# A three-layer forward pass on one core: key and value products put into the heads' pipeline steps, and two small stages moved one step later

## The chip, the cores and the metric

The kernel runs on one core of a Trainium2 chip. The metric is the device time of one execution in microseconds (us). Before the change it is 1878.92 us, the median of 3 runs (1877.95 to 1881.15).

## The reference

A sequence of 512 tokens of width 1024 passes through three mixers, each followed by a feed-forward part. The first mixer is a gated linear recurrence with a convolution of width 4, the second is attention over latent keys with a learned choice of keys, the third is chunked gated linear attention with a pooling branch. The change touches the first and the second. Cut to what matters there:

```
# recurrence: convolution, two gates, scan, output product
gate, xr = split(h @ w_in, 2);  gate = gelu(gate)
xc = conv_b + sum_k xpad[:, k:k+S] * conv_w[k]
r = sigmoid(xc_blocks @ w_a + b_a);  i = sigmoid(xc_blocks @ w_x + b_x)
log_a = -8 * r * softplus(-lam);  a = exp(log_a);  u = sqrt(-expm1(2*log_a)) * (i * xc)
hs = scan(hs*a + u);  y = (hs * gate) @ w_out

# attention: q (16 heads of 64), latent c (128), index queries and keys
c = rms_norm(c, kv_norm_g)
score = sum_h wi_h * relu(qi_h . ki);  idx = top_k(score, 128), per query
logits = q_lat . c[idx] + bias;  p = softmax(logits);  o_lat = p @ c[idx]
o = (o_lat @ w_uv) @ w_o          # q_lat = (q @ w_uk) / 8
```

The kernel multiplies the latent keys by `w_uk` and `w_uv` once (key products `kt`, value products `v`), and takes the choice of keys as a mask that is added to the logits.

## The kernel before

All activations lie transposed, features on 128 partitions and 512 tokens along a row. Every product runs in three matmuls of rounded operands (`group`, lines 348 to 353: high by high, low by high, high by low), so each weight chunk of 128x1024 is split first: ScalarE (ACT) rounds it into `wh` (line 254), VectorE (DVE) or, in the attention, GpSimd (POOL) subtracts to get `wl` (line 255). Activations are split in the same way by `split` (lines 364 and 365). A matmul's result stands in one of eight PSUM banks (`PS`, one pool of eight tiles), and a new product takes the bank of the one eight earlier, once that has been read out.

The order of the work is made by `run` (line 268 on). A job is a list of stages, and job i executes its stage s in step i + s: in each step stage 0 of the newest job comes first, then the later stages of older jobs. A scheduler then lays the instructions out for each engine by priority, so an instruction can move a little, but each engine then works strictly in its order. A stage that waits on an engine holds everything behind it there.

The recurrence. `LAYER0` lists its jobs: eight convolution tiles `xr` 0 to 7 (`conv_job`: product; read-out `xr`; taps, one on ACT and three on DVE, into `xc`; rounding `out_`), four gate pairs `ax` 0 to 3 (`recur_job`: 24 matmuls into four banks; gates `rg` and `ig` on ACT, lines 570 and 571; factors; scan `hs`), and eight output gates `rgate` (24 matmuls each; gelu; product with `hs`; rounding `h`, `l` from `gate`). The rounding of the last tile, `xr` 7, belongs to the same step as the gates of `ax` 1, and stands ahead of them on ACT. `ax` 2 needs the banks that `ax` 1's gates read out; the tile `xr` 7 itself is first needed by `ax` 3. The output product `rout` then reads the eight rounded tiles of `gate`, in order.

The attention. First come the index queries, the keys, the query products `q_job` (read out into `qq`) and the latent keys `c_job` (product; read-out `c` with its squares `csq`; an empty stage; `norm`, a sum over partitions by a matmul `tot` and a reciprocal square root; `out_`, rounding into `C`). The top-k choice runs on DVE as 48 rounds (lines 809 and 810, 16 for each of three query blocks), handed out a few at a time by the jobs. Then 8 key products `kt_job` (3 matmuls, read out by ACT into `kth` and by DVE into `ktl`, then three DMAs on SyncE's queue (SP) into `kto` and `kth`), 8 value products `v_job` (3 matmuls, read out by ACT and DVE into `vv`), and 32 heads `head_job` (16 heads for each half of the queries). A head has nine stages: loads (bias tile `btile`, query copies `qd` by DMA on SP, rounding `qph`, `qpl`); logits; softmax (DVE `probs`, `negmax`; ACT exponent; DVE `sums`; POOL scaling); top-k rounds; two empty ones; transposes `pT`, rounded into `pTh` and `pTl`; an empty one; value products `o`, read out for two heads at once (ACT `olo`, DVE `os`). All jobs stand in one list, one per step: key products 0 and 1, value products 0 and 1, then heads 0 and 1 with the last two query products, then for heads 2 to 4 each head followed by two key and two value products, then heads 5 to 31 alone.

Of the kernel before, what the change touches and what calls it, by code (L numbers as in the profile page):

```python
# [21 lines left out]
KD = D // P  # L22
# [193 lines left out]
def blocks(ap):  # L216
    return ap.rearrange("p (n c) -> p n c", c=P)


def reverse(ap):  # L220
    return blocks(ap)[:, :, ::-1]
# [49 lines left out]
def run(jobs):  # L271

    deep = max(len(j) for j in jobs)
    for step in range(len(jobs) + deep - 1):
        for stage in [0] + list(range(deep - 1, 0, -1)):
            i = step - stage
            if 0 <= i < len(jobs) and stage < len(jobs[i]):
                jobs[i][stage]()


@with_exitstack
def build(ctx, tc, xT, wall, par, relb, onehot, edges, out):
    nc = tc.nc
# [11 lines left out]
    def T(dt=F32, name="t"):  # L295
        return tp.tile([P, S], dt, name=name, tag="t")
# [25 lines left out]
    def pc(name, j=0, n=1):  # L322
        if name == "g_mix0":
            return g0[:, j:j + n]
        c = PCOL[name] + j
        return pt[:, c:c + n]
# [28 lines left out]
    def lin(X, *key):  # L355
        h, l = W.get(*key)
        ps = PS()
        group(ps, [(h[:, k * P:(k + 1) * P], l[:, k * P:(k + 1) * P], X[k][0], X[k][1]) for k in range(KD)])
        return ps

    def split(t):

        h, l = T(F32R, "h"), T(F32R, "l")
        act(h, t, AF.Copy)
        V.tensor_sub(l, t, h.bitcast(F32))
        return h, l
# [9 lines left out]
    def total(acc):  # L376
        ps = PS("tot")
        PE.matmul(ps, ones, acc, start=True, stop=True)
        return ps

    def rsqrt_mean(ps, n):
        s = T(name="std")
        act(s, ps, AF.Sqrt, scale=1.0 / n, bias=eps_t)
        V.reciprocal(s, s)
        return s
# [28 lines left out]
    def residual_job(j, mm, feed, half=False):  # L414
        st = {}

        def first():
            st["ps"] = mm()

        def second():  # L420
            if half:
                stt(xs[j], st["ps"], 0.5, xs[j], op0=ALU.mult, op1=ALU.add)
            else:
                V.tensor_add(xs[j], xs[j], st["ps"])  # L424
            if feed is not None:
                feed.add(xs[j])

        return [first, second]
# [82 lines left out]
    def first_products():  # L511

        first_ps.extend(PS() for _ in range(NFIRST))
        at = {f: i for i, f in enumerate(FIRST)}
        todo = sorted((max(at["x", k], at["w", c, k // 4]), k, c) for k in range(KD) for c in range(NFIRST))
        left = [3 * KD] * NFIRST
        for _, k, c in todo:
            (h, l), (xh, xl) = W.done[c], feed.X[k]
            cols = slice(k * P, (k + 1) * P)
            for a, b in ((h, xh), (h, xl), (l, xh)):  # L520
                left[c] -= 1
                PE.matmul(first_ps[c], a[:, cols], b, start=left[c] == 3 * KD - 1, stop=left[c] == 0)  # L522
        for c in range(NFIRST):
            W.get("xr", c)

    def conv_job(j):
        st = {}

        def mm():
            if j == 0:  # L530
                first_products()
            st["ps"] = first_ps[j] if j < NFIRST else lin(feed.X, "xr", j)

        def evict():
            t = st["t"] = T(name="xr")
            feed.r
            with tc.high_priority(offset=EARLY):
                V.tensor_mul(t, st["ps"], feed.r)

        def taps():  # L540
            t = st["t"]
            c = xc[j] = T(name="xc")
            act(c, t, AF.Identity, scale=pc("conv_w3", j), bias=pc("conv_b", j))
            for k in range(3):
                n = 3 - k
                stt(c[:, n:], t[:, :S - n], pc(f"conv_w{k}", j), c[:, n:], op0=ALU.mult, op1=ALU.add)

        def out_():
            xcs[j] = split(xc[j])

        return [mm] + [lambda: None] * max(0, 2 - j) + [evict, taps, out_]

    def recur_job(b):
        st = {}
# [91 lines left out]
    jobs = [[lambda: None, softplus]]  # L646
# [5 lines left out]
    def rout(j):  # L652

        if j == 0:
            rout_ps.extend(PS() for _ in range(4))
            for kk in range(4):
                h, l = W.get("routk", kk)
                for k in range(2):
                    kt = 2 * kk + k
                    yh, yl = Y[kt]  # L660
                    for i in range(4):
                        c = slice(k * 512 + i * P, k * 512 + (i + 1) * P)
                        PE.matmul(rout_ps[i], h[:, c], yh, start=kt == 0, stop=False)
                        PE.matmul(rout_ps[i], h[:, c], yl, start=False, stop=False)
                        PE.matmul(rout_ps[i], l[:, c], yh, start=False, stop=kt == KD - 1)
        return rout_ps[j] if j < 4 else lin(Y, "rout", j)

    jobs = [residual_job(j, lambda j=j: rout(j), nxt) for j in range(KD)]
# [28 lines left out]
    def qi_job(j):  # L697
        st = {}

        def mm():  # L700
            st["ps"] = lin(feed.X, "att", j)

        def ev():
            t = st["t"] = T(name="qi")
            V.tensor_mul(reverse(t), blocks(st["ps"]), blocks(feed.r))

        def out_():
            for e in range(2):
                qi[2 * j + e] = T(F32R, "qis")
                stack(qi[2 * j + e], st["t"], e, V if j == 0 else G)  # L710

        return [mm, ev, out_]
# [31 lines left out]
    def c_job():  # L744
        st = {}

        def mm():
            st["ps"] = lin(feed.X, "att", 5)

        def ev():  # L750
            c = st["c"] = T(name="c")
            V.tensor_mul(c, st["ps"], feed.r)
            sq = st["sq"] = T(name="csq")
            act(sq, c, AF.Square)

        def norm():
            st["r"] = rsqrt_mean(total(st["sq"]), P)

        def out_():
            c = st["c"]  # L760
            stt(c, c, pc("g_kv"), st["r"], op0=ALU.mult, op1=ALU.mult)
            C.extend(split(c))

        return [mm, ev, lambda: None, norm, out_]

    accs, ready = [None] * 4, [False] * 4

# [48 lines left out]
    def q_job(j):  # L816
        st = {}

        def mm():
            st["ps"] = lin(feed.X, "att", 6 + j)  # L820

        def ev():
            t = QF[j] = T(name="qq")
            stt(reverse(t), blocks(st["ps"]), 0.125, blocks(feed.r), op0=ALU.mult, op1=ALU.mult)

        def more():
            for _ in range(SELECT_PER_Q):
                next(rounds, None)

        return [mm, ev, more]  # L830

    def kt_job(j):
        st = {}

        def mm():
            if j == 0:
                uk.extend(W.get("uk"))
            ps = st["ps"] = PS()
            group(ps, [(uk[0][:, j * P:(j + 1) * P], uk[1][:, j * P:(j + 1) * P], *C)])

        def ev():
            h, l, o = T(F32R, "kth"), T(F32R, "ktl"), T(F32R, "kto")
            act(h, st["ps"], AF.Copy)
            V.tensor_sub(l, st["ps"], h.bitcast(F32))

            for dst, src in ((o[0:64], h[64:P]), (o[64:P], l[64:P]), (h[64:P], l[0:64])):
                nc.sync.dma_start(dst.bitcast(F32), src.bitcast(F32))
            KT[2 * j], KT[2 * j + 1] = h, o

        return [mm, ev]  # L850
# [145 lines left out]
    jobs = [qi_job(j) for j in range(4)] + [kw_job(), q_job(0)]  # L996
# [11 lines left out]
    heads = [head_job(pair, h) for pair in range(2) for h in range(16)]  # L1008

    kts = [kt_job(j) for j in range(8)]  # L1010
    vals = [v_job(kt, n) for kt, n in ((0, 0), (1, 0), (0, 1), (1, 1), (2, 0), (3, 0), (2, 1), (3, 1))]
    jobs += kts[:2] + vals[:2] + [heads[0], q_job(6), heads[1], q_job(7)]
    for i in range(2, 8, 2):
        jobs += [heads[i // 2 + 1]] + kts[i:i + 2] + vals[i:i + 2]

    def further():
        W.limit = len(W.plan)
        W.fetch(W.at + W.ahead)

    run(jobs + heads[5:10] + [[further]] + heads[10:])  # L1020

    nxt = Feed("g_mlp1")

# [48 lines left out]
    def lr_job():  # L1072
        st = {}

        def mm():
            st["ps"] = lin(feed.X, "lr")

        def ev():
            t = T(name="lr")
            V.tensor_mul(t, st["ps"], feed.r)  # L1080
            LR.extend(split(t))

        return [mm, ev]
# [315 lines left out]
    jobs = [lr_job(), [lambda: None, halves], k_job(0), k_job(1), k_job(2)]  # L1399
# [114 lines left out]
    jobs = [last_job(d, full, first, n, hid) for d in range(KD - 4)]  # L1514
# [39 lines left out]
```

## Time and profile before

| | us |
|---|---|
| median of 3 runs | 1878.92 |
| the profiled execution | 1878.08 |
| its span, first to last instruction | 1876.1 |
| TensorE (PE) busy | 1838.0 |
| DVE busy | 1020.1 |
| ACT busy | 807.4 |
| POOL busy | 201.4 |

The recurrence lies at about 7 to 150 us of the span, the attention with its heads at about 550 to 735 us. A busy PE in the profile is one that has a matmul under way; a 128x512 matmul is listed with 0.39 us, but the next one starts 0.23 us after it, since they overlap. The granted clock (PEclk) says how much of its full speed TensorE was given in a stretch. A row of a timeline gives the start in us from the beginning of the span, the duration, engine and line, and in brackets the idle time of the engine just before, with what ended it.

### The profile page before, as it was taken

To read this page: it belongs to the slowest core of one execution; us is meant where nothing else is said; L and a number is where in the kernel's file an instruction comes from. 1 tells how busy PE (TensorE), PEld (TensorE's weight loads), DVE (VectorE), ACT (ScalarE), POOL (GpSimd) and SP (SyncE) were. 2 spreads that over 40 slices of the span, in tenths; PEclk is the share of its full clock that TensorE was granted. 3 is DMA by queue.
4 is the path that set the end of the run, shared out by engine and by line. 5 is a ranking of instruction groups with operands and counts; after the bars stand their busy time and mean duration, and the time that the engine had idled before them with its cause. 6 is when DMAs were issued, how large, how long until landed. Compare 5 with 4: busy or idle time off the path is not lost.

```text
span 1876.1 us, 21800 instructions
## 1 busy us (share of the span) xinstructions
PE 1838.0 (98%) x8450; PEld 1522.8 (81%) x8450; DVE 1020.1 (54%) x1504; ACT 807.4 (43%) x1224; POOL 201.4 (11%) x202
## 2 busy tenths in 40 slices
PE   9899999999999689999999999999999999999998
PEld 7788888888887578888888888888888888888887
DVE  7787542443359987543244444736585554344344
ACT  6794431343344586442134445356542333122233
POOL 0000000000165465000000023401000000000000
PEclk9999999999999899999999999999999999999999
DMA  5223222222233531222222222221122222222221
GB/s 200 84 90 103 101 90 101 96 96 101 90 101 111 143 90 40 101 99 92 101 93 99 101 90 100 92 90 57 60 98 94 97 100 92 101 95 95 102 75 60
DMA packets 60999, 179.36 MB, mean 96 GB/s; under 512 B 7696, under 2 KB 18144, under 8 KB 60896
## 3 DMA queue, kind: packets, MB, share of 16 engines
q1 hardware_dynamic: 60752, 177.97, 28.1%
q8 instruction: 66, 1.08, 0.2%
q14 instruction: 37, 0.30, 0.1%
q10 hardware_dynamic: 144, 0.00, 0.0%
HBM read 168.48 MB, written 2.12 MB: 91 GB/s over the span
## 4 chain that ended last, share of the span: by engine, by line
PE 91%; DVE 5%; ACT 2%; DMA 1%; issue 1%; POOL 0%; SPq 0%; DVEq 0%; ACTq 0%; POOLq 0%
PE ps L351 19%; PE ps L353 19%; PE ps L352 19%; PE dn L352 8%; PE dn L353 8%; PE dn L351 8%; DVE score L810 1%; PE o L1317 1%; DVE top L809 1%; PE ps L522 1%; PE v L1222 1%; PE v L1223 1%; PE v L1224 1%; DVE score L791 1%; PE kv L1291 1%
## 5 line engine op out<-in xcount | busy, mean ns | idle before, releaser
L254 ACT ACTIVATE wh<-wst 128x1024 fp32r<-128x1024 f32 (+2 forms) x314 | 328.0, 1046 | 897.3 <-PE ps L352 364.0
L351 PE MATMUL ps<-xh,wh 128*128 128x512 f32 x1376 | 540.8, 393 | 0.0
L353 PE MATMUL ps<-xh,wl 128*128 128x512 f32 x1376 | 535.3, 389 | 0.0
L352 PE MATMUL ps<-xl,wh 128*128 128x512 f32 x1376 | 535.2, 389 | 0.0
L255 DVE TENSOR_TENSOR wl<-wst,wh 128x1024 fp32r<-128x1024 f32 (+2 forms) x283 | 342.6, 1211 | 221.6 <-ACT wh L254 194.8
L352 PEld LDWEIGHTS ps<-xl,wh 128*128 128x128 f32 x1376 | 258.3, 188 | 55.9 <-issue 2.4
L351 PEld LDWEIGHTS ps<-xh,wh 128*128 128x128 f32 x1376 | 258.3, 188 | 55.5 <-issue 2.2
L353 PEld LDWEIGHTS ps<-xh,wl 128*128 128x128 f32 x1376 | 258.3, 188 | 53.7
L351 PE MATMUL dn<-h,wh 128*128 128x512 f32 (+1 forms) x712 | 271.8, 382 | 0.0
L352 PE MATMUL dn<-l,wh 128*128 128x512 f32 (+1 forms) x712 | 271.7, 382 | 0.0
L353 PE MATMUL dn<-h,wl 128*128 128x512 f32 (+1 forms) x712 | 271.7, 382 | 0.0
L255 POOL TENSOR_TENSOR wl<-wst,wh 128x1024 fp32r<-128x1024 f32 x31 | 75.8, 2452 | 916.6 <-ACT wh L254 916.4
L351 PEld LDWEIGHTS dn<-h,wh 128*128 128x128 f32 x712 | 133.8, 188 | 26.1
L352 PEld LDWEIGHTS dn<-l,wh 128*128 128x128 f32 x712 | 133.8, 188 | 25.9
L353 PEld LDWEIGHTS dn<-h,wl 128*128 128x128 f32 x712 | 133.8, 188 | 25.7
L424 DVE TENSOR_TENSOR x<-x,dn 128x512 f32<-128x512 f32 x48 | 33.0, 688 | 170.7 <-PE dn L353 170.7
L455 DVE SCALAR_TENSOR_TENSOR relu<-ps,std 128x512 f32<-128x512 f32 x64 | 44.2, 691 | 146.8 <-PE ps L353 146.7
L351 PE MATMUL ps<-h,wh 128*128 128x512 f32 x200 | 78.7, 396 | 5.4 <-ACT rg L570 5.4
L352 PE MATMUL ps<-l,wh 128*128 128x512 f32 x200 | 78.8, 394 | 0.0
L353 PE MATMUL ps<-h,wl 128*128 128x512 f32 x200 | 78.6, 393 | 0.0
L351 PEld LDWEIGHTS ps<-h,wh 128*128 128x128 f32 x200 | 38.0, 190 | 14.5 <-ACT rg L570 6.3
L1501 DVE TENSOR_TENSOR u<-ps,std 128x512 f32<-128x512 f32 x22 | 15.2, 690 | 62.5 <-PE ps L353 62.5
(315 smaller groups left out, 2128.2 us busy)
## 6 DMA issues: line engine op xcount, KB each, us to landing
wst<-wall SPq DMA_DIRECT2D x300, 512.0 KB, 3.2
btile<-biasdram SPq DMA_DIRECT2D x32, 128.0 KB, 3.1
qd<-qq SPq DMA_DIRECT2D x64, 64.0 KB, 2.2
wst<-wall SPq DMA_DIRECT2D x8, 384.0 KB, 2.9
x<-xT SPq DMA_DIRECT2D x8, 256.0 KB, 5.2
out_dram<-fin SPq DMA_DIRECT2D x8, 256.0 KB, 2.3
wst<-wall SPq DMA_DIRECT2D x6, 256.0 KB, 5.1
kto<-kth SPq DMA_DIRECT2D x8, 128.0 KB, 3.0
```

The lines of the kernel that those rows point to most:

```text
L254: self.nc.scalar.activation(h[:, a:b], st[:, a:b], AF.Copy)
L255: eng.tensor_sub(l[:, a:b], st[:, a:b], h[:, a:b].bitcast(F32))
L351: PE.matmul(ps, wh, xh, start=i == 0, stop=False)
L352: PE.matmul(ps, wh, xl, start=False, stop=False)
L353: PE.matmul(ps, wl, xh, start=False, stop=i == n - 1)
L424: V.tensor_add(xs[j], xs[j], st["ps"])
L455: stt(t, st["ps"], 0.0, feed.r, op0=ALU.max, op1=ALU.mult)
L522: PE.matmul(first_ps[c], a[:, cols], b, start=left[c] == 3 * KD - 1, stop=left[c] == 0)
L791: stt(accs[i][:, :w], d[:, :w], sg, accs[i][:, :w], op0=ALU.mult, op1=ALU.add)
L809: V.max(top, acc[:, :w])
L810: V.match_replace(acc[:, :w], top, acc[:, :w], MARK)
L1222: PE.matmul(st["ps"][i], xh, hk, start=kt == 0, stop=False)
```

## The change

Four edits, all of them in which step a stage falls.

The rounding of the convolution's last tile gets an empty stage ahead of it. The norm of the latent keys gets a second empty stage ahead of it. A new function `together` merges jobs into one that executes their stages of the same number in one step. With it, key products 0 and 1 share a step; value products 0 and 1 share the step of head 0's loads; then query product 6; head 1 with key products 2 and 3; query product 7; and heads 2 to 6 each with two more products (value 2 and 3; key 4 and 5; key 6 and 7; value 4 and 5; value 6 and 7). Heads 7 to 31 stand alone as before. No instruction is added or taken away.

```
+def together(*jobs):
+
+    deep = max(len(j) for j in jobs)
+    return [lambda n=n: [j[n]() for j in jobs if n < len(j)] for n in range(deep)]
...
-        return [mm] + [lambda: None] * max(0, 2 - j) + [evict, taps, out_]
+        return [mm] + [lambda: None] * max(0, 2 - j) + [evict, taps] + [lambda: None] * (j == KD - 1) + [out_]
...
-        return [mm, ev, lambda: None, norm, out_]
+        return [mm, ev, lambda: None, lambda: None, norm, out_]
...
-    jobs += kts[:2] + vals[:2] + [heads[0], q_job(6), heads[1], q_job(7)]
-    for i in range(2, 8, 2):
-        jobs += [heads[i // 2 + 1]] + kts[i:i + 2] + vals[i:i + 2]
+    jobs += [together(*kts[:2]), together(heads[0], *vals[:2]), q_job(6), together(heads[1], *kts[2:4]), q_job(7)]
+    beside = (vals[2:4], kts[4:6], kts[6:8], vals[4:6], vals[6:8])
+    jobs += [together(heads[i + 2], *b) for i, b in enumerate(beside)]
...
-    run(jobs + heads[5:10] + [[further]] + heads[10:])
+    run(jobs + heads[7:10] + [[further]] + heads[10:])
```

The lines of the changed kernel are counted six higher from `run` on. On ACT, in the recurrence, this stands before the gates of `ax` 1 (`rg`, `ig`), first before the change:

```order
L614 ACTIVATE gate<-gate 128x512
L254 ACTIVATE wh<-wst 128x1024
L598 ACTIVATE q<-q,minus 128x512 x2
L364 ACTIVATE h<-xc 128x512
L570 ACTIVATE rg<-ps,half_b 128x512
L571 ACTIVATE ig<-ps,half_b 128x512
L570 ACTIVATE rg<-ps,half_b 128x512
L571 ACTIVATE ig<-ps,half_b 128x512
L577 ACT_TABLE_LOAD
L577 ACTIVATE q<-rg,sp_n 128x512 x2
```

And at the same place with it:

```order
L620 ACTIVATE gate<-gate 128x512
L254 ACTIVATE wh<-wst 128x1024
L604 ACTIVATE q<-q,minus 128x512 x2
L576 ACTIVATE rg<-ps,half_b 128x512
L577 ACTIVATE ig<-ps,half_b 128x512
L576 ACTIVATE rg<-ps,half_b 128x512
L577 ACTIVATE ig<-ps,half_b 128x512
L583 ACT_TABLE_LOAD
L583 ACTIVATE q<-rg,sp_n 128x512 x2
L370 ACTIVATE h<-xc 128x512
```

The rounding `h<-xc` of tile 7 has moved from ahead of the four gates to behind the two exponentials that follow them.

On DVE, in the attention, these rows hold the softmaxes of heads 6 to 8 before the change (`probs`, `negmax`; two rows of `probs` are one head; `pTl` is the rounding of an earlier head's transposes, `top` and `score` are top-k rounds):

```order
L936 ISA probs,negmax<-logit,btile 128x128
L936 ISA negmax 128x1
L936 ISA probs,negmax<-logit,btile 128x256
L936 ISA negmax 128x1
L809 MAX top<-score 128x8
L936 ISA probs,negmax<-logit,btile 128x128
L936 ISA negmax 128x1
L936 ISA probs,negmax<-logit,btile 128x256
L936 ISA negmax 128x1
L936 ISA probs,negmax<-logit,btile 128x128
L936 ISA negmax 128x1
L936 ISA probs,negmax<-logit,btile 128x256
```

And the softmaxes of heads 7 and 8 with it:

```order
L966 TENSOR_TENSOR pTl<-pT,pTh 128x384
L942 ISA probs,negmax<-logit,btile 128x128
L942 ISA negmax 128x1
L942 ISA probs,negmax<-logit,btile 128x256
L942 ISA negmax 128x1
L815 MAX top<-score 128x8
L947 RECIPROCAL sums<-sums 128x2
L966 TENSOR_TENSOR pTl<-pT,pTh 128x384
L942 ISA probs,negmax<-logit,btile 128x128
L942 ISA negmax 128x1
L942 ISA probs,negmax<-logit,btile 128x256
```

Before, the softmaxes of heads 5 to 8 stand in a row with half a round of top-k between them and no `pTl`; now each of heads 6 to 12 has at least one `pTl` between its softmax and the one before. The last `probs` of a head and its own `pTl` are further apart, and the end of the top-k choice, which stood behind head 10's softmax, stands behind head 12's. From head 14's softmax on the rows of DVE are the same in both.

## Rows read from the trace of the kernel before

**Rows 1.** The page, part 1: busy us, share of the span, instructions.

```profile
PE 1838.0 (98%) x8450; PEld 1522.8 (81%) x8450; DVE 1020.1 (54%) x1504; ACT 807.4 (43%) x1224; POOL 201.4 (11%) x202
```

**Rows 2.** Waits of PE, whole span: us in total, times, longest us.

```profile
PE pT L956 <- POOL probs L944: 8.2, 6, 3.5
PE ps L351 <- ACT rg L570: 5.4, 2, 4.0
PE o L972 <- ACT pTh L959: 4.8, 8, 1.6
...
PE o L973 <- DVE pTl L960: 3.3, 4, 1.7
PE tot L378 <- ACT csq L754: 1.3, 1, 1.3
```

**Rows 3.** Timeline of PE: start us, us, what, [idle before <- releaser].

```profile
66.60 0.50 PE L351 MATMUL ps<-h,wh 128*128 128x512 f32 x1 [1.43 <-ACT rg L570]
66.94 0.40 PE L352 MATMUL ps<-l,wh 128*128 128x512 f32 x1
...
82.86 0.39 PE L353 MATMUL ps<-h,wl 128*128 128x512 f32 x1
87.24 0.77 PE L351 MATMUL ps<-h,wh 128*128 128x512 f32 x1 [3.99 <-ACT rg L570]
87.81 0.63 PE L352 MATMUL ps<-l,wh 128*128 128x512 f32 x1
...
91.00 0.39 PE L351 MATMUL ps<-h,wh 128*128 128x512 f32 x1
...
105.29 0.40 PE L351 MATMUL ps<-h,wh 128*128 128x512 f32 x1
...
145.20 0.39 PE L664 MATMUL ps<-l,wh 128*128 128x512 f32 x1
```

**Rows 4.** Timeline of ACT around the gates of ax 1 and ax 2.

```profile
81.94 1.32 ACT L598 ACTIVATE q<-q,minus 128x512 f32<-128x512 f32 x2
85.98 0.63 ACT L364 ACTIVATE h<-xc 128x512 fp32r<-128x512 f32 x1 [2.73 <-DVE xc L546]
86.52 0.67 ACT L570 ACTIVATE rg<-ps,half_b 128x512 f32<-128x512 f32 x1
...
104.35 0.67 ACT L570 ACTIVATE rg<-ps,half_b 128x512 f32<-128x512 f32 x1
```

**Rows 5.** Timeline of DVE: last tap of tile 7; low part of gate 5.

```profile
85.16 0.73 DVE L546 SCALAR_TENSOR_TENSOR xc<-xr,params,xc 128x511 f32<-128x511 f32 x1
...
143.40 0.67 DVE L365 TENSOR_TENSOR l<-gate,h 128x512 fp32r<-128x512 f32 x1
```

**Rows 6.** Stretches: us, busy us of each engine, PEclk, DMA share, GB/s.

```profile
92.00:125.00 33.00, 33.00 (x147) 27.32 (x146) 29.92 (x40) 32.83 (x46) 0.00 (x0) 1.00 0.25 84
557.00:649.00 92.00, 77.04 (x356) 61.41 (x354) 89.61 (x238) 44.17 (x94) 43.23 (x34) 0.94 0.44 126
649.00:671.00 22.00, 17.10 (x102) 14.43 (x103) 16.86 (x66) 17.57 (x60) 15.89 (x27) 0.84 0.48 115
671.00:725.00 54.00, 49.80 (x344) 43.46 (x343) 47.48 (x137) 48.68 (x126) 34.55 (x51) 1.00 0.22 54
```

**Rows 7.** Waits of DVE from 649 to 671 us.

```profile
DVE os L979 <- ACT olo L977: 1.7, 2, 1.4
DVE sums L941 <- ACT probs L939: 1.4, 3, 0.7
DVE pTl L960 <- ACT pTh L959: 1.2, 2, 0.7
DVE pTl L960 <- POOL qpl L894: 0.5, 1, 0.5
```

**Rows 8.** Timeline of DVE: low part of the latent keys c.

```profile
589.88 2.33 DVE L365 TENSOR_TENSOR l<-c,h 128x512 fp32r<-128x512 f32 x1
```

**Rows 9.** Timeline of POOL at the same time.

```profile
589.25 2.41 POOL L255 TENSOR_TENSOR wl<-wst,wh 128x1024 fp32r<-128x1024 f32 x1 [7.33 <-ACT wh L254]
```

## The prediction

> **What bounds the kernel now.** I read the page's first part, then the waits of PE, then the timelines of the two places that the change touches, then the busy time of the engines by stretch. The page shows a kernel that is bound by TensorE: 1838.0 of 1876.1 us are PE busy [rows 1]. So the only time that a change of order can give back is where PE stands still or runs at half clock, and the list of PE's waits says where that is [rows 2]: 5.4 us in the recurrence on `rg`, in two waits, and otherwise the attention, on `probs`, `pTh` and `pTl`. All of these places are touched.
>
> In the recurrence the reader is to see one chain. PE issues its last matmul at 82.86, and its next at 87.24, with 3.99 us idle, released by an `rg` [rows 3]. That is the third of `ax` 2's four banks, which `ax` 1's first gate has to read out. ACT did not run this gate late for want of data: it was free at 83.26 (81.94 + 1.32), then stood 2.73 us behind `h<-xc`, the rounding of tile 7, which waited for a DVE tap, and ran the gate at 86.52 [rows 4]. The tap started at 85.16 [rows 5]. The stop cost more than its length: from 87.24 to 91.00 nine matmuls follow each other in 3.76 us, 0.42 apart, PE's level of 1.2 GHz. All matmuls together take 0.218 each (1838.0 / 8450, [rows 1]); at that pace, and with 0.34 for the first as behind the earlier stop (66.60 to 66.94), nine are 2.1 to 2.2 us, so 1.6 us are lost on top. The shorter stop before 66.60 (1.43 us) left no such trace: the second matmul takes 0.40, against 0.63 behind the long stop [rows 3].
>
> In the attention PE is not the limit. From 557 to 649 us DVE is busy 89.6 of 92.0 us, PE 77.0; from 649 to 671 DVE 16.9 of 22.0; from 671 to 725 DVE 47.5 and PE 49.8 of 54.0 [rows 6]. DVE first holds the rest up, then has gaps of its own, then both are nearly full.
>
> **The rounding one step later.** Nothing is added; on ACT one instruction of 0.54 us (85.98 to 86.52) moves behind two exponentials. The four gates can start at 83.26 instead of 86.52, 3.26 earlier. The first ends some 0.6 later, and PE starts again at about 83.95 instead of 87.24: 3.3 us gained, and the 1.6 us at half clock with it, if a stop of 0.9 us is as harmless as the one of 1.43. PE then stands 4.9 us ahead.
>
> It cannot keep all of it, because ACT is full from here on: 32.83 of 33.00 us between 92 and 125 [rows 6]. The gates of `ax` 2 came at 104.35 [rows 4]. They come 3.26 earlier and 0.54 later, as the rounding now lies in between: 101.63, and the first one is read out by 102.25. PE needs that bank for the third product of `ax` 3, at 105.29 before [rows 3] and 4.9 earlier now, 100.4. In the kernel before this fitted by 0.3 us; now PE waits 1.8 us and goes on at 102.25, 3.0 us ahead. The next narrow place is the output product: the matmul with the low part of gate 5 started at 145.20 [rows 3], that low part was written from 143.40 to 144.07 [rows 5], a slack of 1.1 us. PE's new order brings this matmul five matmuls (1.1 us) forward, and DVE's chain gains no more than ACT's 2.7. So another 0.4 us are waited for. What stays is 2.6 us. Bounds: 4.9 if ACT finds time somewhere, and a loss of 0.5 if the gates start no earlier and the rounding only lengthens ACT's chain. I take 2.6, the sum by the rows. The rounding's own reader, `ax` 3, is some 13 us behind it, so its cover is wide.
>
> The Trainium skill, in "TensorE: Matmul & The Clock Gate", section "What's actually happening", says that the throttled state is the default and activity releases it. The stop of 3.99 us agrees, with matmuls 0.42 apart behind it. It speaks against the gain: the new wait of 1.8 us at `ax` 3 is one that the old kernel did not have. If it threw the clock back as the long stop did, 1.6 us would go and the 2.6 would be 1.0.
>
> **The norm of the latent keys one step later.** PE's wait of 1.3 us on the squares [rows 2] should shrink or go. I credit nothing: it lies at 580 us, in the stretch in which DVE is the full engine and PE has 15 us to spare, so PE meets DVE again a little later. Bounds: 0 and a gain of 1.3. The low part of the keys took 2.33 us on DVE [rows 8], against 0.67 for the same operation and shape elsewhere [rows 5], while POOL had a subtraction under way until 591.66 [rows 9]. Since DVE is full, 1.7 us would be gained if the moved work fell into a pause of POOL, and as much lost if another one fell into POOL's way. I take nothing.
>
> The Trainium skill, "SBUF — State Buffer", section "Who interferes with whom", explains this row: a DVE instruction with two inputs in SBUF and a POOL instruction that reads SBUF lock each other out, whoever comes first. The trace agrees (2.33 us, ending 0.6 behind POOL's instruction). By the rule the loss may come back at the new place, so the sum by it is the same zero, between -1.7 and +1.7.
>
> **Products beside heads.** No instruction is added, so DVE's work stays what it is: the 89.6 us of the first stretch cannot shrink by order alone. What can shrink is the 5.1 us that DVE idles between 649 and 671 (22.0 - 16.9). Their causes are latencies of one head [rows 7]: `olo` 1.7, `sums` 1.4, `pTh` 1.2, and 0.5 that goes with `pTl`. They arise because DVE has worked off products and top-k rounds by then, takes four softmaxes in a row and comes to the transposes of the same heads before exponent, scaling and transposes have run. In the new order the heads come in early with one product pair each, the top-k rounds last until behind head 12's softmax instead of head 10's (the order of DVE above), and each head's `pTl` lies further behind its softmax. From head 14 on DVE's rows are the same as before, so the 6.5 us of idle time from 671 to 725 stay. Of the 5.1 us I leave about 1.2, the waits around heads 10 to 12, where the distance hardly grows, and take 3.9. Bounds: the whole 5.1 as a gain, and a loss as in the third rival below. SP's queue is moved as well: a later head's query copies now stand ahead of the first key copies. I cost that at nothing, since DVE reads the first odd head's logits later than before, behind the products that now stand beside head 0; if this cover is too thin, DVE waits there once, at most for the issue and landing of those copies.
>
> **The sum.** The profiled execution took 1878.08 us, 0.84 under the median of 1878.92. 2.6 + 0 + 3.9 = 6.5 us less gives 1871.6 for it, and 1872.4 beside the median. What a measurement of this kernel tells from no change is about 0.2%, 3.8 us.
>
> **Rivals.**
> 1. The heads gain nothing: DVE's gaps move behind head 14, where the rows are unchanged, since PE and DVE are both near full there (49.8 and 47.5 of 54.0). For it: that stretch takes heads at its own pace. Against it: what lies ahead of it can start it earlier. Only the recurrence counts: 1878.9 - 2.6 = 1876.3, no change by the measure above.
> 2. More comes back: the recurrence keeps its 4.9 us, the heads all 5.1 and the keys' low part its 1.7. For it: PE's half-clock spells in the heads (mean granted clock 0.84 from 649 to 671) could go too. Against it: ACT's full 33 us. 1878.9 - 11.7 = 1867.2.
> 3. Slower, by banks. Two products now stand in the same step as each of heads 3 to 6, and their banks are free only when DVE, the full engine, has read them. PE works in order, so the logits and transposes queued behind a product that waits for a bank come late, DVE runs out of softmaxes, and the stall feeds itself. Price: a wait like those of PE on `probs`, 1.4 us in the mean and 3.5 at most [rows 2], once in each of the four steps: 5.5 to 14.0. I take 8, nearer the mean: 1878.9 - 2.6 + 8 = 1884.3. It decides from 6.4 us of such waits that DVE shares; a wait of PE alone costs nothing here. Against it: before, four products stood one behind the other between two heads as well, and DVE was still full. The Trainium skill names the pattern in "Perfetto Trace Analysis", section "Optimization Strategy" (repeated gaps on an engine that should be full can mean too little PSUM); no row here shows a bank wait in the heads.
> 4. The rounding's move does nothing: another instruction holds ACT ahead of the gates. The new order shows none; it would cost the 2.6 and give 1875.0 with the heads' gain.
>
> **How the numbers follow.** I give the forecast 0.46, the first rival 0.19, the second 0.15, the third 0.12, the fourth 0.08. The forecast's own range is 1869 to 1875. The range for 8 in 10 takes in the first and fourth rival and most of the second, and leaves out the third: 1866.5 to 1879. Faster by over 0.2%: forecast and second rival, with half of the fourth: 0.65. Within 0.2%: first rival, half of the fourth: 0.22. Slower: 0.13.
>
> **What would show it.** Right: PE's wait before `ax` 2's third bank falls under 1.2 us without half-clock matmuls behind it, and a new one of 1 to 2 us appears at `ax` 3 on `rg`; the output product starts 2 to 3 us earlier; DVE as full as before up to head 8, its idle time between heads 8 and 14 down to about 1 us, and the head stage's end some 4 us earlier against the recurrence's end. Wrong: a wait of ACT behind some other tap or of `ax` 3 for the rounding; DVE idle before head 8; PE waiting on `ktl` or `vv` among the heads; or the same gain in front of head 14 lost again behind it.

## The result and the profile after

The changed kernel takes 1869.29 us in the median (1868.5 to 1870.22), the kernel before 1879.76 beside it: ratio 0.9945, 95% interval 0.9928 to 0.9962. By the ratio that is 10.3 us less (7.1 to 13.5); 1872.4 was forecast, with 1866.5 to 1879 as its range. The two profiled executions, from which all positions below are taken, took 1878.08 and 1870.07, 8.0 us apart, with spans of 1876.1 and 1868.3, 7.8 us apart.

The first part of the page and the list of PE's waits, which answer to [rows 1, 2]:

```profile
PE 1836.4 (98%) x8450; PEld 1521.9 (81%) x8450; DVE 1016.9 (54%) x1504; ACT 806.8 (43%) x1224; POOL 201.3 (11%) x202
...
PE ps L357 <- ACT rg L576: 4.2, 3, 2.2
PE o L978 <- ACT pTh L965: 3.6, 6, 1.5
PE pT L962 <- POOL probs L950: 3.5, 4, 1.3
PE logit L931 <- DVE pTl L966: 2.8, 3, 2.3
...
PE logit L931 <- DVE ktl L850: 1.4, 1, 1.4
```

The wait on `rg` is shorter but now comes three times, the waits on `probs` fell from 8.2 to 3.5 us, `logit` waits for `pTl` and `ktl`, which it did hardly or not at all before, and DVE, which does the same 1504 instructions, is busy 3.2 us less.

**The recurrence.** PE's timeline, answering to [rows 3]:

```profile
83.58 0.50 PE L357 MATMUL ps<-h,wh 128*128 128x512 f32 x1 [0.63 <-ACT rg L576]
83.92 0.40 PE L358 MATMUL ps<-l,wh 128*128 128x512 f32 x1
...
102.36 0.50 PE L357 MATMUL ps<-h,wh 128*128 128x512 f32 x1 [2.17 <-ACT rg L576]
102.70 0.39 PE L358 MATMUL ps<-l,wh 128*128 128x512 f32 x1
...
103.67 0.63 PE L359 MATMUL ps<-h,wl 128*128 128x512 f32 x1
...
106.65 0.55 PE L357 MATMUL ps<-xh,wh 128*128 128x512 f32 x1
107.04 0.39 PE L358 MATMUL ps<-xl,wh 128*128 128x512 f32 x1
```

And ACT's, answering to [rows 4]:

```profile
81.64 1.32 ACT L604 ACTIVATE q<-q,minus 128x512 f32<-128x512 f32 x2
82.86 0.66 ACT L576 ACTIVATE rg<-ps,half_b 128x512 f32<-128x512 f32 x1
...
88.00 0.62 ACT L370 ACTIVATE h<-xc 128x512 fp32r<-128x512 f32 x1
...
101.65 0.67 ACT L576 ACTIVATE rg<-ps,half_b 128x512 f32<-128x512 f32 x1
```

The long stop of 3.99 us has shrunk to 0.63, and the matmuls behind it run at full pace. The gates of `ax` 2 come at 101.65, and PE stops for them at `ax` 3, until 102.36. Behind that stop PE first runs at full pace, then falls to its level of 1.2 GHz from 103.67 to 107.04: eight matmuls, 0.42 apart, at a mean granted clock of 0.51.

**The attention.** The stretches, with columns as in [rows 6]: from the same point of the attention's start to head 0's first softmax, from there to head 6's, and from there to head 16's. First before the change:

```profile
557.00:609.41 52.41, 51.13 (x230) 41.78 (x229) 50.73 (x120) 23.45 (x38) 26.77 (x16) 1.00 0.35 109
609.41:647.00 37.59, 25.41 (x124) 19.27 (x123) 36.88 (x108) 20.10 (x54) 16.47 (x18) 0.86 0.56 151
647.00:671.44 24.44, 18.04 (x110) 15.22 (x110) 19.30 (x79) 18.63 (x64) 16.33 (x28) 0.86 0.48 114
```

And with it:

```profile
555.78:608.58 52.80, 51.97 (x234) 42.67 (x233) 51.04 (x127) 24.07 (x39) 26.88 (x16) 1.00 0.37 115
608.58:638.25 29.67, 22.35 (x112) 17.04 (x111) 29.42 (x90) 19.04 (x54) 16.47 (x19) 0.83 0.56 138
638.25:663.80 25.55, 18.52 (x117) 14.98 (x117) 24.22 (x89) 18.45 (x60) 15.80 (x27) 0.93 0.54 154
```

The three together took 114.44 us and take 108.02. DVE's busy time (the third of the engines' times) summed to 106.91 and sums to 104.68, so its idle time fell from 7.5 to 3.3 us. Of the 6.4 us 4.2 are idle time, and 2.2 are work that is the same work. Of DVE's waits in the last stretch, answering to [rows 7], one of note is left:

```profile
DVE pTl L966 <- ACT pTh L965: 0.7, 1, 0.7
```

Two instructions hold 1.9 of the 2.2 us. The first is the addition of the causal triangle to the last scores, before:

```profile
605.89 1.88 DVE L796 TENSOR_TENSOR score<-score,tri 128x128 f32<-128x128 f32 x1
...
605.22 2.40 POOL L255 TENSOR_TENSOR wl<-wst,wh 128x1024 fp32r<-128x1024 f32 x1
```

With the change, and the keys' low part beside it, answering to [rows 8]:

```profile
588.55 2.02 DVE L371 TENSOR_TENSOR l<-c,h 128x512 fp32r<-128x512 f32 x1
...
601.25 0.28 DVE L802 TENSOR_TENSOR score<-score,tri 128x128 f32<-128x128 f32 x1
```

Before, the addition began while POOL subtracted, and ended at 607.77, where POOL's instruction ended at 607.62. Now it falls into a pause of POOL and takes 0.28 us. This is the lock that the Trainium skill describes in "SBUF — State Buffer", section "Who interferes with whom": a DVE instruction with two inputs in SBUF waits for a POOL instruction that reads SBUF and came first. The trace agrees here as at the keys' low part.

### The profile page after: what moved, and what is told of

Same layout as the page of the kernel before. It is cut to its first block, busy times and chain, and to the rows that moved or that the text cites. A ratio compares the mean times of both kernels' runs of the same rounds, so it can differ in the third digit from the quotient of the medians.

```text
span 1868.3 us, 21802 instructions
## 1 busy us (share of the span) xinstructions
PE 1836.4 (98%) x8450; PEld 1521.9 (81%) x8450; DVE 1016.9 (54%) x1504; ACT 806.8 (43%) x1224; POOL 201.3 (11%) x202
## 4 chain that ended last, share of the span: by engine, by line
PE 89%; DVE 6%; ACT 2%; issue 1%; DMA 0%; POOL 0%; SPq 0%; DVEq 0%; ACTq 0%; POOLq 0%
PE ps L357 18%; PE ps L359 18%; PE ps L358 18%; PE dn L359 8%; PE dn L357 8%; PE dn L358 8%; DVE score L816 1%; DVE top L815 1%; PE o L1323 1%; PE ps L528 1%; PE v L1229 1%; PE v L1228 1%; PE v L1230 1%; DVE score L797 1%; PE kv L1297 1%
```

## Experiments

Each kernel's edit is set against the kernel before unless said otherwise. The table has the median, the ratio to the kernel before with its interval, and, from the one profiled execution of each, three numbers. "Recurrence" is the time from the matmul behind PE's first stop (66.60 before) to DVE's first `qi` of the attention (534.09 before), "attention" that from there to head 16's first softmax (671.44 before), both against the kernel before, whose own are 467.49 and 137.35. "Half clock" counts the matmuls behind the stop that the row names whose next one starts over 0.36 us later; the first behind the stop is left out, since it is longer at either clock (0.33 to 0.60). How far such a stretch moves from one schedule to the next by itself, e1 shows: its attention is 1.09 us longer, and its edit doesn't touch the attention. So a difference of about 1 us in the last column is not to be put down to an edit by that column alone.

| kernel | median | ratio | recurrence | stop; half clock | attention |
|---|---|---|---|---|---|
| before | | | 0 | 3.99; 7 | 0 |
| changed | 1869.29 | 0.9945 (0.9928 to 0.9962) | -0.94 | 2.17; 8 | -6.42 |
| e1 rounding | 1878.45 | 0.9999 (0.9990 to 1.0007) | -0.86 | 2.13; 8 | +1.09 |
| e2 norm | 1877.88 | 0.9997 (0.9988 to 1.0006) | +0.98 | 4.01; 12 | -0.07 |
| e3 products | 1875.91 | 0.9984 (0.9975 to 0.9993) | -0.06 | 3.98; 5 | -0.82 |
| e4 changed, gates on POOL | 1869.08 | 0.9951 (0.9938 to 0.9963) | -3.02 | 1.09; 0 | -5.67 |
| e5 norm, products | 1873.49 | 0.9971 (0.9960 to 0.9982) | +0.89 | 4.01; 11 | -5.87 |
| e6 rounding, products | 1874.62 | 0.9978 (0.9969 to 0.9988) | -0.89 | 2.17; 8 | -0.91 |
| e7 copies early | 1879.18 | 1.0001 (0.9993 to 1.0010) | +1.22 | 4.01; 13 | +1.03 |
| e8 changed, copies early | 1873.23 | 0.9966 (0.9955 to 0.9977) | -2.50 | 2.13; 0 | -3.58 |
| e9 products, weights by POOL | 1873.30 | 0.9970 (0.9958 to 0.9981) | +0.03 | 3.99; 8 | -4.43 |
| e10 changed, weights by POOL | 1872.07 | 0.9963 (0.9950 to 0.9977) | -2.51 | 2.17; 0 | -3.03 |
| e11 e4 and e10 together | 1872.06 | 0.9962 (0.9950 to 0.9975) | -3.05 | 1.05; 0 | -2.88 |

**e1 rounding: the first edit alone.**

```
-        return [mm] + [lambda: None] * max(0, 2 - j) + [evict, taps, out_]
+        return [mm] + [lambda: None] * max(0, 2 - j) + [evict, taps] + [lambda: None] * (j == KD - 1) + [out_]
```

> The kernel before with the first edit alone: tile 7's rounding one step later. Theory: all that the recurrence gives comes from this edit, 0.9 us (1.6 of half clock and 3.3 of waiting are gained behind the first stop, 2.2 of waiting and 1.6 of half clock are lost at the next one). PE waits for rg three times, 1.4, 0.6 and 2.2 us, has about nine matmuls 0.42 apart behind the last, and from 125 us on is 0.9 us ahead of the kernel before, counted from the first conv matmuls; time ratio 0.9995, not to be told from 1 by a few rounds. Rival A (the sum of the prediction): 2.6 us ahead, ratio 0.9986. Rival B: the edit gives nothing and the 0.9 us come from elsewhere: 0.0.

The recurrence went as the theory says, 0.86 us. The attention of this execution was 1.09 longer, and no gain shows in the time. The eleven timed runs lie far apart, and with the mean granted clock of the run: the shortest took 1874.8 at 0.993, the three longest 1880.3 to 1880.7 at 0.989.

**e2 norm: the second edit alone.**

```
-        return [mm, ev, lambda: None, norm, out_]
+        return [mm, ev, lambda: None, lambda: None, norm, out_]
```

> The kernel before with the second edit alone: the norm of the latent keys one step later. Theory: 0 us within 0.5, since DVE is the full engine there; PE's wait for the squares goes from 1.3 to under 0.9. Rival: this edit moves the addition of the causal triangle to the scores (1.88 us in the slowest of three on DVE before) out of POOL's way, so that all three take about 0.28 us, and gives 1.6 us by itself, ratio 0.9991. Second rival: the low part of the keys collides with more of POOL's work, and it is 0.5 to 1.7 us slower.

The triangle addition took 0.28 us and the low part 2.02, as in the changed kernel, and DVE reached head 0 in 2.1 us less. From head 0 to head 6 it lost 3.1 again: among others, one `pTl` waits 1.9 us for `pTh`. The rival was right on the instruction and wrong on the gain: work saved on DVE came back as idle time (9.6 us in the three stretches, against 7.5).

**e3 products: the third edit alone** (`together`, and the job list with it).

> The kernel before with the third edit alone: products beside heads. Theory: nearly all of the attention's gain, 5.5 to 6.2 us (ratio 0.9967 to 0.9971): DVE's idle time from the stage's start to head 16's first softmax falls by 4.1 us (from 7.5 to about 3.4) and its busy time by 1.6, as the triangle addition no longer collides with POOL. Rival A: only the 4.1 us of idle time belong to this edit and the collision goes with the norm's move: ratio 0.9978 and one triangle addition of over 1.5 us on DVE. Rival B: it needs the later norm, and gives under 2 us alone.

The theory and rival A missed: DVE's idle time stayed as before (7.4 us in the same three stretches). Rival B came nearest: the attention gained 0.8 us in the profiled execution, and the medians lie 2.8 us apart (3.0 by the ratio, 1.3 to 4.7). In the profile the loss is in one place:

```profile
653.08 0.56 DVE L966 TENSOR_TENSOR pTl<-pT,pTh 128x384 fp32r<-128x384 f32 x1 [2.53 <-DMA qd<-qq]
```

No matmul starts between 650.94 and 653.70, and no activation between 651.13 and 655.28: a query copy is late. SP's queue shows what stands ahead of the copies, two weight transfers:

```profile
643.97 0.87 SPq L248 DMA_DIRECT2D wst<-wall  x2
644.94 0.38 SPq L915 DMA_DIRECT2D btile<-biasdram  x1
645.42 0.56 SPq L894 DMA_DIRECT2D qd<-qq  x1
```

And these are the copies in that stretch (the last line is from issue to landing):

```profile
L894 SPq DMA_DIRECT2D qd<-qq x13: 467/588/1466, 639.4 to 653.8; - x13
...
  DVE pTl L966: 2.5, 1
...
DMA to landing us min/median/max: 1.9/2.0/7.0
```

**e4: the changed kernel, three gate roundings on POOL.**

```
-            Y[j] = split(st["t"])
+            if j < 3:
+                h, l = T(F32R, "h"), T(F32R, "l")
+                G.tensor_copy(h, st["t"])
+                V.tensor_sub(l, st["t"], h.bitcast(F32))
+                Y[j] = h, l
+            else:
+                Y[j] = split(st["t"])
```

> The changed kernel, with the rounding of the first three gate tiles to their high part moved from ACT to POOL, which has nothing to do there. Two of them stand ahead of ax 2's gates on ACT, 0.52 us each. Theory (ACT's full queue sets the wait at ax 3, and the half clock comes from the wait's length): the gates start 1.0 us earlier, PE's wait there falls from 2.2 to about 1.1 us, the nine matmuls behind it are at full clock (1.6 us), and the kernel is 2.4 to 2.7 us faster than the changed kernel, 12.8 us under the kernel before (ratio 0.9932). Rival A: the wait falls, but the half clock stays: 1.0 us faster than the changed kernel. Rival B: POOL's casts hold DVE up, whose taps and scans feed the gates: no gain or a loss of up to 2 us against the changed kernel.

In the code `G` is POOL and `V` is DVE. In the recurrence the theory holds: the stop fell to 1.09, no matmul behind it is at half clock, and 2.1 us more were gained than in the changed kernel. The time is that of the changed kernel all the same; 0.75 us went in the attention, the rest of this is open. (Two of the changed kernel's four timed runs may have had no half clock there either, by the granted clocks given further down; that was not shown.)

**e5 and e6: two edits at a time.** e5 leaves the rounding as before, e6 the norm.

> The kernel before with the second and the third edit (later norm, products beside heads), the rounding as before. The edits alone gave 0.8 and 2.8 us, so their sum would be 3.5. Theory: they act together, because the later norm puts the key products' work and so SP's key copies into another order, and query copies queued behind key copies come on time: 6 to 7 us under the kernel before (ratio 0.9963 to 0.9968), DVE idle under 4.5 us from the attention's start to head 16's first softmax (7.5 before, 7.5 with products alone), and no wait of ACT for query copies over 0.3 us. Rival: the effects add up: 3.5 us (ratio 0.9981) and idle time of DVE over 6 us.

> The kernel before with the first and the third edit (rounding later, products beside heads), the norm as before. Theory: the attention goes as with products alone, and the recurrence gives its 0.9 us: 3 to 4 us under the kernel before (ratio 0.9979 to 0.9984), with ACT's wait for query copies and DVE idle over 6 us to head 16's first softmax. Rival: it is the rounding's edit that makes the heads fast, by moving the attention against the weight transfers: 8 us or more, ratio under 0.996.

Both theories hold in the profile: norm and products gain 5.87 us together in the attention, and 0.07 and 0.82 alone, and e6 gains what products and rounding gave. The times fall just outside what was expected, 5.2 us by the medians in e5 and 4.1 in e6; by the medians norm and products alone gave 0.8 and 2.8, so the excess of the two together is 1.7 us there and 5.0 in the profiles. That they act together the profiles show; how much it is worth stays open. The reason that e5's theory gives, late key copies, is not what the traces show. In e6 `pTl` waits 3.1 us for a query copy, with two weight transfers at 643.50; in e5, as in the changed kernel, three weight transfers are issued together (at 640.30, and 637.94), and no wait for a copy is over 0.4 us. The four copies behind them land no sooner: 5.6 to 6.9 us after their issue in the changed kernel, 4.7 to 7.0 in e3. But the transfers come 0.3 us ahead of head 6's first softmax there and 2.7 us behind it in e3, and nothing has to wait for them.

**e7 and e8: query copies one pair of heads earlier**, in the kernel before and in the changed one.

```
-            if e == 0 and n + 3 < 16:
-                copies((n + 3) // 8, (n + 3) % 8)
+            if e == 0 and n + 4 < 16:
+                copies((n + 4) // 8, (n + 4) % 8)
...
+        if j == 5:
+            jobs.append([lambda: None, lambda: copies(0, 3)])
```

> The kernel before, with each head pair's query copies issued one pair of heads earlier, and nothing else. Theory (part of DVE's idle time ahead of head 16 comes from query copies that stand on SP's queue behind key copies, which wait for DVE): ACT's wait of 1.4 us for them goes, the exponentials of heads 6 to 9 come on time, DVE's idle time to head 16's first softmax falls from 7.5 to about 5, and the kernel is 1.4 to 3 us faster (ratio 0.9984 to 0.9993). Rival (the prediction's: the idle time is the latency of one head from softmax to transposes): the wait on the copies goes, but DVE waits for the next thing of the same head, and the time is the same within 0.5 us.

> The changed kernel, with the query copies issued one pair of heads earlier. Theory: ACT has no wait for query copies over 0.3 us in the changed kernel, so nothing is gained: the same as the changed kernel within 0.7 us, ratio 0.994 to 0.9955 against the kernel before. Rival: copies further ahead still free time of the heads, and it is 1 to 2 us faster than the changed kernel, ratio under 0.994.

e7's theory fell: ACT's wait of 1.4 us for the copies went, and nothing was gained. It is no clean test, though: the added job for the first early copies takes a step of its own, and head 0's first softmax comes 2.5 us later in the attention (3.9 in e8), behind more of DVE's other work. DVE's waits between head 0's and head 16's softmax are now those of single heads:

```profile
DVE pTl L966 <- ACT pTh L965: 3.3, 4, 1.1
DVE os L985 <- ACT olo L983: 1.3, 2, 1.0
```

e8 is 3.9 us slower than the changed kernel by the medians, though the intervals of their ratios touch; both expectations missed. Its loss lies ahead of head 0's softmax, where the added step falls; from there to head 16 it takes 54.1 us against 55.2.

**e9 to e11: three weight transfers from POOL's queue.**

```
...
-        self.nc.sync.dma_start(st[:, a:b], src[:, a:b])
+        eng = self.nc.gpsimd if key in (("wo", 5), ("wo", 6), ("wo", 7)) else self.nc.sync
+        eng.dma_start(st[:, a:b], src[:, a:b])
...
```

> The kernel with products beside heads alone, and the last three of the attention's output weights transferred from POOL's queue in place of SP's. In the kernel with products alone, two of these transfers of 512 KB stand on SP's queue at 643.97, right ahead of four query copies, which land up to 7.0 us after their issue; at 653.08 DVE's pTl waits 2.53 us for such a copy, and PE, ACT and POOL stand still with it. Theory (the transfers ahead of the query copies cost the products their gain): the wait goes, the stretch from head 6's to head 16's first softmax shortens from 29.6 to about 27 us, and the kernel is 2 to 3 us faster than with products alone (1873 to 1874 us, ratio 0.997 to 0.9975). Rival A: the copies share the DMA engines with the weights on whatever queue, and still land late: the same as products alone, ratio 0.9984. Rival B: POOL's issues hold up its scaling of the probabilities, 0.5 to 1 us each: 1 to 2 us slower than with products alone.

e9 met its theory: the copies land in at most 4.3 us, the longest wait that the trace lists with them there is 1.1 us (POOL's, behind ACT's rounding of one), the stretch from head 6 to head 16 is 25.87 us against 29.58 in e3, and the time is 2.6 us less than with products alone.

```profile
L895 SPq DMA_DIRECT2D qd<-qq x14: 467/589/1418, 639.8 to 655.9; - x14
...
DMA to landing us min/median/max: 2.0/2.4/4.3
...
557.56:611.93 54.37, 53.09 (x240) 43.42 (x238) 52.57 (x128) 23.97 (x39) 26.77 (x16) 1.00 0.38 114
611.93:641.70 29.77, 20.97 (x101) 15.73 (x100) 29.12 (x88) 18.49 (x52) 18.42 (x22) 0.82 0.73 173
641.70:667.57 25.87, 20.91 (x123) 18.10 (x122) 24.40 (x90) 19.17 (x62) 15.78 (x26) 0.81 0.42 106
```

The Trainium skill, "DMA: Bandwidth & Descriptors", section "Issuing engines are not separate DMA queues", says that transfers interleave on the same 16 engines whatever engine started them. e9 doesn't contradict it, since its transfers also start earlier, from 619.26 to 630.33. e10 below agrees with it: beside the transfers from POOL's queue its query copies issued from 612 to 640 land in 2.8 us in the median and 4.4 at most, those of the changed kernel at that place in 2.0 and 2.8. So the earlier time is the likelier cure of e3 than the other queue, but no run here parts the two.

> The changed kernel with the same three transfers from POOL's queue. There the three stand on SP's queue at 637.94, and nothing waits for the query copies behind them. Theory: no change against the changed kernel within 0.7 us (ratio 0.9942 to 0.995). Rival: POOL's issues cost what they take, 1 to 2 us slower.

> The changed kernel with the first three gate roundings on POOL, and the three weight transfers from POOL's queue. With the roundings on POOL the recurrence was 1.5 us further ahead than in the changed kernel, and the attention 0.7 us longer, with a wait of DVE for a query copy of 0.6 us. Theory: that wait goes, and the two gains add: 1867.5 to 1868.5 us (ratio 0.994 to 0.9946), a little faster than the changed kernel. Rival: the attention absorbs what the recurrence gives, since it is paced by its own DVE work and transfers, but a constant amount of work cannot absorb an earlier start: the same as the changed kernel within 0.5 us.

Both missed, by about 3 us to the slow side by the medians (the intervals of their ratios overlap the changed kernel's). In e10 POOL issues the transfers at 614.51, 619.17 and 626.22, where copies of keys and queries run densest, and ACT waits 2.4 us for query copies there that it did not wait for in the changed kernel:

```profile
L895 SPq DMA_DIRECT2D qd<-qq x17: 467/594/1690, 613.0 to 644.1; - x17
...
  ACT qph L900: 2.4, 2
```

So the transfers of the weights cost the attention about 3 us in the profiles (2.8 to 3.6 between e3 and e9, the changed kernel and e10, e4 and e11) or nothing, by where they fall.

## Why the prediction was right, and where it was not

The time and its sign were right, from a sum whose terms were partly off. Against 6.5 us forecast for the profiled execution stand 7.8 by the spans: 0.3 ahead of the recurrence, where nothing was changed, 0.94 + 6.42, and 0.2 behind. That the sum came near is partly luck: the recurrence gave 1.7 less than forecast and the attention 2.5 more.

**Rounding, 2.6 forecast, 0.94 measured.** Every step up to the new wait came as worked out: PE resumed at 83.58 (83.95), the gates of `ax` 2 at 101.65 (101.63), PE at `ax` 3 at 102.36 (102.25). (All of this trace lies 0.28 us earlier than the one before; set against that, the gates came 0.3 us late.) What failed is that this wait was taken as harmless: it is 2.17 us long, not 1.8, and about 1.6 us at half clock followed. The prediction had worked out this case too, to 1.0 us. It did so beside what the Trainium skill says in "TensorE: Matmul & The Clock Gate", section "What's actually happening", that the throttled state is the default and activity releases it; the trace agrees here, with the granted clock of 0.51 behind the stop. That price is not fixed. Stops of 0.63 to 1.43 us never had it here. Behind five stops of 2.13 to 2.17 us it came three times (changed, e1, e6) and stayed away twice (e8, e10), where the recurrence gained 2.5, the sum as forecast. In e8, at the same place:

```profile
102.96 0.50 PE L357 MATMUL ps<-h,wh 128*128 128x512 f32 x1 [2.13 <-ACT rg L576]
...
104.22 0.39 PE L359 MATMUL ps<-h,wl 128*128 128x512 f32 x1
104.45 0.40 PE L357 MATMUL ps<-h,wh 128*128 128x512 f32 x1
```

Behind the six stops of 3.98 to 4.01 us it was 5 to 13 matmuls. Over these profiles the edit is worth 2.0 us in the mean (-1.54 over five kernels that differ there in nothing else, +0.51 over six without it); that is one execution of each, and e1's time shows 0.2 us, at most 1.9. The further wait at the output product, 0.4 in the sum, did not come. e4 shows that ACT's queue was the limit, as argued.

**Norm, 0 forecast.** The low part of the keys still met POOL (2.33 to 2.02 us). What I did not read is the triangle addition, 1.88 us in one of three equal instructions; the later norm frees it, and e2, e4, e5 and e8, which have that edit too, show 0.28 and 2.02 as well. Alone this is worth nothing (e2). Beside the products it shows as 1.3 us less of DVE's work (e9 to e5), of which the two instructions hold 0.8, since the addition takes only 0.80 to 0.82 with the old norm there (e3, e6, e9). Its larger worth, which the prediction did not see, is that it takes the weight transfers out of the products' way, as said next.

**Products, 3.9 forecast, 4.2 of DVE's idle time measured.** The size came out: from head 6 to head 16, where the 3.9 was sought, the idle time fell from 5.1 to 1.3 us. The reason given for the idle time before, latencies of single heads and not the copies, agrees with the waits that went and with those left in e7, but e7 is no clean test of it.

But the edit alone gave 0.8 us in the profile (2.8 by the medians), which no step foresaw. The step that prices the moved queue of SP, "I cost that at nothing", held for the four edits together and fails for this one alone, and it looked at key copies only. With the old norm, weight transfers fall ahead of query copies at a worse time, and a wait of 2.5 us and its followers eat the gain; with these transfers elsewhere, products alone give 4.43 (e9; 5.4 by the medians). That the later norm came with the products was thus luck for the forecast. The remaining 1.4 us to e5's 5.87 are for the most part DVE's shorter instructions: 106.1 us of work in e9's three stretches, 104.8 in e5's. The norm's move cures the transfers only by shifting the order. Why the `pTl` instruction has to wait for a query copy the trace does not say; most likely its buffer, from the one pool that all such tiles share, held the `qq` that the copy reads.

**Rivals.** The third, banks, shows its sign without its price: `logit` waits 2.3 us for a `pTl` and 1.4 for a `ktl`, instructions that read banks out, as the prediction named for a wrong outcome, but DVE had other work meanwhile and is idle less than before, so a wait of PE alone cost nothing. Its price counts heads 3 to 6, while by the code two products stand beside each of heads 0 to 6. The first is excluded by the attention's 6.42, of which nothing is lost behind head 16. The second's time (1867.2) is nearer to the measured one than the forecast's, 2.1 us against 3.1, but two of its three gains did not come: the recurrence gave 0.94 of 4.9, the keys' low part 0.3 of 1.7. The fourth is excluded by the gates, which start at 82.86, as soon as ACT is free.

The timed difference of 10.3 is above the 7.8 of the profiles by 2.5, of which the scatter of the half clock is the only source seen. The granted clocks of the timed runs fit: the changed kernel's took 1868.5 twice at 0.996, and 1870.1 and 1870.2 at 0.994 and 0.995, about the price of one spell, and e1's runs lie apart in the same way. Which stop had a spell in those runs no trace shows.

No version beat the changed kernel by more than the measurement tells; e4 equals it.

## What to carry to other kernels

Here a stall removed from a full engine's queue came back at the next place where that queue was late. So follow the chain to there, and price the new stop with its half clock as a chance and not as a sum. Where one engine is full, look for single instructions that take several times their usual time, beside what POOL does then. When the order of work changes, place the large transfers on the new timeline too: in this kernel the same edit was worth 0.8 or 4.4 us in the profiles, 2.8 or 5.4 by the medians, by where three of them fell and on which queue. And test an edit together with the others as well as alone.

## What the runs showed of the hardware

Stops of PE of the same length (2.13 to 2.17 us), at the same place in the program, were followed by eight matmuls at 1.2 GHz in three kernels and by none in two. A DVE addition of 128x128 took 0.28 us by itself, and 0.80 to 1.88 us where it began under a subtraction of POOL, by how much of that was left (before, e1, e3, e6, e7, e9). Copies of 64 KB that land in 2.0 us in the median took up to 7.0 behind two transfers of 512 KB (e3) and up to 6.9 behind three (changed). In e3 DVE stood still for 2.5 us with them, in the changed kernel nothing waited over 0.2 us.
